# Values of sixteen meta tokens: both parts of the activations side by side as one stationary operand

## The chip, the cores and the metric

The kernel runs on one core of a Trainium2 chip. The metric is the device time in microseconds, taken as the median of several runs. TensorE multiplies matrices into PSUM, VectorE (DVE) and ScalarE (ACT) read PSUM and SBUF, GpSimd (POOL) reads SBUF alone, and DMA queues bring the weights from HBM.

## What is computed

A trunk of two layers over 16 learned meta tokens and 512 frames, each a vector of 1024. Each layer is a half-step feed-forward block, a mixer of three groups of heads (pooling, convolution, retention) and a second feed-forward block, each with a residual and a layer norm. The change is in the mixer, where the retention heads get their values `v` from the combined input projection:

```python
def token_mix(h, w_in, ..., w_out):
    z = h @ w_in
    xp, ca, cg, q, k, v, g = jnp.split(z, splits, axis=-1)
    y_pool = pool_mixer(xp, pool_w, pool_scale)
    y_conv = conv_module(ca, cg, conv_dw, conv_db, conv_ln_g, conv_ln_b, conv_pw)
    y_ret = retention(q, k, v, g, ret_gn_g)
    return jnp.concatenate([y_pool, y_conv, y_ret], axis=-1) @ w_out
```

In `retention` each of four heads of width 128 forms scores of `q` and `k` with decays, applies them to `v`, and normalizes the result over the head.

## The kernel before

All numbers are float32. For the matrix products each operand is split into a high part in fp32r and the remainder as a low part; a product is three matmuls: high by high, high by low and low by high (`mm3`, lines 130 to 135). `weights` (line 86) loads a block of weights, ScalarE casts the high part (line 91), VectorE subtracts it (line 94). Activations stand transposed: eight tiles `xs[k]` of 128 features, each in two halves of 264 columns (256 frames and 8 meta tokens), each half a pair of high and low part.

The mixer (`mixer`, from line 566) first projects the inputs of the convolution and of the pooling. Then it makes the values, the part that the change touches. `xm` gathers the meta tokens' 8 + 8 columns of both halves with small copies on GpSimd (line 670), four for each of eight feature tiles. Five passes over `tt` follow: four of 128 frames and, for `tt == 4`, one of the 16 meta tokens. A pass runs over eight feature tiles; the activations are the stationary operand, the weights' high and low parts the moving one of 512 columns, three matmuls for each tile (lines 680 to 682), 24 in a pass. Behind a pass VectorE sums the 512 columns of a row by heads (line 684) and scales by -1/128 (line 685), and ScalarE copies each head out of PSUM with that shift, four copies (line 690).

Then `work(hd, before)` makes, head by head, keys, gates and queries (`project`, `rotary`, lines 701 to 705). Each key half gives its 8 meta columns to the tile `km` by a copy on GpSimd (line 794). `attend` runs the score products (line 719; the first has `km` as its stationary operand), their decays (line 730), and the products with the values (line 738). Between these steps the 62 taps of the causal convolution are handed out on VectorE, one line 610 each, by the generator `conv_taps`, first asked for a tap within this loop.

The code's text isn't the order on the engines: a planner runs through the program with its own times for every instruction and puts on each engine, when that is free, the earliest instruction of the text whose inputs are there. That order is then fixed. Tiles of one tag share a number of buffers: `acc` has 4 PSUM banks (used by value passes, keys, queries and gates in turn), `wide` 16, the high and low parts of weights 5 each, `xm` 8.

Of the kernel before, what the change touches and what calls it, by code (L numbers as in the profile page):

```python
# [10 lines left out]
F32R = mybir.dt.float32r  # L11
I32 = mybir.dt.int32
AF = mybir.ActivationFunctionType
ALU = mybir.AluOpType
PSUM = bass.MemoryType.PSUM

P = 128
D = 1024
KT = D // P
SEQ = 512  # L20
NM = 16
# [24 lines left out]
HM = NM // 2  # L46
NT = 256 + HM
# [11 lines left out]
def trunk(ctx, tc, a):  # L59
    nc = tc.nc  # L60
# [3 lines left out]
    sq_pool = ctx.enter_context(tc.tile_pool(name="seqp", bufs=1))  # L64
    pp = ctx.enter_context(tc.tile_pool(name="pp", bufs=1, space=PSUM))

    def t(name, tag, dt=F32):
        return tp.tile([P, NT], dt, tag=tag, name=name, bufs=TILES[tag])

    def acc(name, tag="acc"):  # L70
        return pp.tile([P, 512], F32, tag=tag, name=name, bufs=BANKS[tag])
# [4 lines left out]
    def raw(r):  # L76
        return r.bitcast(F32)
# [42 lines left out]
    def wide(name, dt=F32):  # L120
        return sq_pool.tile([P, WIDE], dt, tag="wide", name=name, bufs=WIDES)
# [15 lines left out]
    def at(pair, sl):  # L137
        return pair[0][:, sl], pair[1][:, sl]
# [12 lines left out]
    xs = [[None, None] for _ in range(KT)]  # L151
# [214 lines left out]
    def project(ws, s, n, name):  # L366

        ps = [acc(f"{name}_{i}") for i in range(len(ws))]
        for k in range(KT):
            for w, p_ in zip(ws, ps):  # L370
                mm3(p_[:, :n], at(w, slice(k * P, (k + 1) * P)), at(xs[k][s], slice(0, n)), k == 0, k == KT - 1)
        return ps
# [193 lines left out]
    def mixer(l, name):  # L566
# [13 lines left out]
        for (kind, c), s in in_two([("u", 0), ("u", 1), ("xp", 0), ("xp", 1)], 3):  # L580
            n = ns[s]
            if s == 0:
                tiles = (c, 2 + c) if kind == "u" else (4 + c,)
                ws[kind, c] = [weights(w_in[i], 1024, f"{name}w{i}") for i in tiles]
                p_ = pad if kind == "u" else ppad
                seq[kind, c] = wide(f"{name}{kind}{c}")[:, : p_ + L]
                nc.gpsimd.memset(seq[kind, c][:, :p_], 0.0)  # L587
            ps = project(ws[kind, c], s, n, f"{name}p{kind}{c}{s}")
# [75 lines left out]

        xm = []
        for k in range(KT):
            pair = sq_pool.tile([P, 2, NM], F32R, tag="xm", name=f"{name}xm{k}", bufs=KT)
            for p_ in range(2):
                for s in range(2):
                    nc.gpsimd.tensor_copy(pair[:, p_, s * HM : (s + 1) * HM], raw(xs[k][s][p_][:, 256:NT]))  # L670
            xm.append((pair[:, 0, :], pair[:, 1, :]))
        vt = {}
        wv = [weights(a["w_v"][l, j], 1024, f"{name}wv{j}") for j in range(4)]
        for tt in range(5):
            n = NM if tt == 4 else P
            ps = acc(f"{name}v{tt}")
            for k in range(KT):
                xh, xl = xm[k] if tt == 4 else at(xs[k][tt // 2], slice(tt % 2 * P, (tt % 2 + 1) * P))
                wh, wl = at(wv[k // 2], slice((k % 2) * 512, (k % 2 + 1) * 512))
                nc.tensor.matmul(ps[:n], lhsT=xh, rhs=wh, start=k == 0, stop=False)  # L680
                nc.tensor.matmul(ps[:n], lhsT=xh, rhs=wl, start=False, stop=False)
                nc.tensor.matmul(ps[:n], lhsT=xl, rhs=wh, start=False, stop=k == KT - 1)
            mu = sq_pool.tile([P, HEADS], F32, tag="vmu", name=f"{name}vmu{tt}", bufs=2)
            nc.vector.tensor_reduce(out=mu[:n], in_=ps[:n].rearrange("p (h e) -> p h e", h=HEADS), axis=mybir.AxisListType.X, op=ALU.add)
            nc.vector.tensor_scalar(out=mu[:n], in0=mu[:n], scalar1=-1.0 / P, scalar2=None, op0=ALU.mult)
            for hd in range(HEADS):
                if hd % 2 == 0:
                    vc = t(f"{name}vc{tt}{hd}", "h")
                sl = slice((hd % 2) * P, (hd % 2 + 1) * P)
                nc.scalar.activation(vc[:n, sl], ps[:n, hd * P : (hd + 1) * P], AF.Identity, bias=mu[:n, hd : hd + 1])  # L690
                vt[tt, hd] = vc[:n, sl]
# [280 lines left out]
    for l in range(DEPTH):  # L972
        ffn(0, l, (NT, NT), f"f{l}a", V_LN + 3 * l * 16, {(1, 0): lambda: (load_tokens((2, 3, 5)), enter(1)), (0, 1): lambda: turn(1)} if l == 0 else {})
        if l == 0:
            with tc.issue_after(entered["ffn"]):
                load_mixer_constants()
        mixer(l, f"m{l}")
        if l < DEPTH - 1:
            ffn(1, l, (NT, NT), f"f{l}b", V_LN + (3 * l + 2) * 16)
        else:  # L980
            last_ffn(l, f"f{l}b")
# [92 lines left out]
```

## Time and profile before

| | us |
|---|---|
| median of 3 runs | 1978.54 |
| lowest and highest | 1976.29 and 1979.73 |
| profiled execution, its own time | 1979.3 |
| its span, first to last instruction | 1977.5 |
| TensorE busy | 1912.4 (97%) |
| VectorE busy | 1548.9 (78%) |
| ScalarE busy | 920.1 (47%) |
| GpSimd busy | 215.0 (11%) |

The prediction's rows come from the page of the profiled execution and from views of its trace: the waits (who waited for whom, and how long), the timeline (instructions of an engine in order of time, neighbours of one kind merged), and tables of busy time by stretches. Times count from the span's start. Layer 0's value passes lie at 427 to 455 us, layer 1's at 1405 to 1433. TensorE's weight loads (PEld) run beside its matmuls. A matmul's duration is longer than the distance to the next, since they are pipelined.

### The profile page before, as it was taken

How to read it: one execution, taken by the hardware profiler on the slowest of the kernel's cores; microseconds unless marked ns; L12 is line 12 of the kernel's file. 1: busy time of each engine (PE TensorE's matmuls, PEld its weight loads, DVE VectorE, ACT ScalarE, POOL GpSimd, SP SyncE). 2: the span in 40 equal slices, each digit the busy share in tenths (PEclk: the TensorE clock that was granted, in tenths of full speed). 3: DMA queues.
4: the chain of work that ended last, by engine and by line, in shares of the span. 5: the costliest groups of instructions: out<-in, count | busy, mean ns of one | idle time of the engine just before them, and what ended most of it. 6: DMA issues, size and time to landing. Idle time of an engine off the chain costs nothing.

```text
span 1977.5 us, 36739 instructions
## 1 busy us (share of the span) xinstructions
PE 1912.4 (97%) x14423; PEld 1826.3 (92%) x14423; DVE 1548.9 (78%) x3466; ACT 920.1 (47%) x1845; POOL 215.0 (11%) x283
## 2 busy tenths in 40 slices
PE   7999999999999999999999999999999999999996
PEld 6999999997899899999989999998889998999995
DVE  7788778689767977788697787787897697877787
ACT  5454446443333644454464554464343265544451
POOL 4000000442003000000120000005320130000001
PEclk9999999999999999999999999999999999999998
DMA  4422323322112233323213323332131213323321
GB/s 143 129 86 97 116 88 104 100 76 85 63 34 75 64 98 108 97 89 107 95 54 111 101 89 107 97 118 75 65 104 54 65 44 118 107 86 107 107 97 43
DMA packets 61069, 177.98 MB, mean 90 GB/s; under 512 B 6976, under 2 KB 10944, under 8 KB 60896
## 3 DMA queue, kind: packets, MB, share of 16 engines
q1 hardware_dynamic: 59744, 174.59, 27.8%
q8 instruction: 113, 1.85, 0.4%
q10 hardware_dynamic: 1152, 1.05, 0.2%
q14 instruction: 60, 0.49, 0.1%
HBM read 173.52 MB, written 2.10 MB: 89 GB/s over the span
## 4 chain that ended last, share of the span: by engine, by line
PE 79%; DVE 12%; POOL 3%; issue 3%; ACT 2%; DMA 0%; SPq 0%; DVEq 0%; POOLq 0%; ACTq 0%
PE f0a_y L134 2%; PE f0a_y L133 2%; PE f1bo L890 2%; PE f1bo L888 2%; PE f0a_y L135 2%; PE f1bo L889 2%; PE f0b_y L134 2%; PE f1a_y L134 2%; PE f0b_y L133 2%; PE f0b_y L135 2%; PE f1a_y L135 2%; PE f1a_y L133 2%; DVE m0y L610 1%; DVE m1y L610 1%; PE m0sc L719 1%
## 5 line engine op out<-in xcount | busy, mean ns | idle before, releaser
L610 DVE SCALAR_TENSOR_TENSOR m1y<-m1u,vec,m1y 128x528 f32<-128x528 f32 x60 | 46.1, 801 | 0.0
L91 ACT CAST f0a_o_h<-f0a_o_r 128x512 fp32r<-128x512 f32 (+1 forms) x37 | 23.5, 635 | 48.4 <-PE f0a_y L134 29.5
L610 DVE SCALAR_TENSOR_TENSOR m0y<-m0u,vec,m0y 128x528 f32<-128x528 f32 x60 | 45.9, 801 | 0.0
L91 ACT CAST f1a_o_h<-f1a_o_r 128x512 fp32r<-128x512 f32 (+1 forms) x37 | 23.6, 637 | 48.0 <-PE f1a_y L134 29.0
L91 ACT CAST f0b_o_h<-f0b_o_r 128x512 fp32r<-128x512 f32 (+1 forms) x37 | 23.5, 636 | 47.6 <-PE f0b_y L134 29.3
L335 DVE TENSOR_TENSOR x<-x,f0a_y 128x264 f32<-128x264 f32 x64 | 27.1, 425 | 23.3 <-PE f0a_y L135 23.1
L335 DVE TENSOR_TENSOR h<-h,f0b_y 128x264 f32<-128x264 f32 x64 | 27.1, 425 | 23.2 <-PE f0b_y L135 23.1
L335 DVE TENSOR_TENSOR h<-h,f1a_y 128x264 f32<-128x264 f32 x64 | 27.1, 424 | 23.1 <-PE f1a_y L135 23.0
L94 DVE TENSOR_TENSOR f1bw_l<-f1bw_r,f1bw_h 128x512 fp32r<-128x512 f32 x42 | 27.7, 688 | 17.6 <-ACT f1bw_h L91 17.0
L949 POOL TENSOR_TENSOR yt<-yt,g_last 128x256 f32<-128x256 f32 x4 | 3.0, 740 | 337.2 <-ACT yt L948 337.2
L94 DVE TENSOR_TENSOR f0a_o_l<-f0a_o_r,f0a_o_h 128x512 fp32r<-128x512 f32 (+1 forms) x42 | 26.6, 642 | 13.4 <-ACT f0a_o_h L91 11.3
L94 DVE TENSOR_TENSOR f1a_o_l<-f1a_o_r,f1a_o_h 128x512 fp32r<-128x512 f32 (+1 forms) x42 | 26.7, 642 | 13.4 <-ACT f1a_o_h L91 11.4
L94 DVE TENSOR_TENSOR f0b_o_l<-f0b_o_r,f0b_o_h 128x512 fp32r<-128x512 f32 (+1 forms) x42 | 26.7, 642 | 12.6 <-ACT f0b_o_h L91 10.4
L278 POOL TENSOR_TENSOR f0b_ln_s<-h,h 128x264 f32<-128x264 f32 x2 | 1.6, 820 | 313.8 <-DVE h L335 313.8
L587 POOL MEMSET m1u<- 128x30 f32 x2 | 0.2, 123 | 307.6 <-PE f1a_20Q L135 307.6
L587 POOL MEMSET m0u<- 128x30 f32 x2 | 0.2, 123 | 306.1 <-PE f0a_20Q L135 306.1
L91 ACT CAST f1bw_h<-f1bw_r 128x1024 fp32r<-128x1024 f32 (+1 forms) x22 | 22.2, 1011 | 21.0 <-PE f1bo L890 4.2
L894 DVE TENSOR_TENSOR yt<-yt,f1bo 128x256 f32<-128x256 f32 x80 | 27.8, 414 | 5.4 <-PE f1bo L890 5.3
L291 ACT ACTIVATE m_ln_q<-h 128x264 f32<-128x264 f32 (+1 forms) x32 | 11.9, 414 | 39.7 <-DVE h L289 36.1
L257 PE MATMUL tr<-ident,xtok 128*128 128x128 f32 (+1 forms) x48 | 10.9, 328 | 12.1 <-DVE xtok L242 11.4
L281 POOL TENSOR_TENSOR m_ln_s<-m_ln_s,h 128x264 f32<-128x264 f32 (+1 forms) x20 | 18.2, 912 | 32.0 <-DVE h L329 26.1
L257 PEld LDWEIGHTS tr<-ident,xtok 128*128 128x128 f32 (+1 forms) x48 | 6.8, 167 | 16.1 <-issue 14.8
(10805 smaller groups left out, 9335.0 us busy)
## 6 DMA issues: line engine op xcount, KB each, us to landing
f1bw_r<-in_w2last SPq DMA_DIRECT2D x20, 512.0 KB, 3.8
f0a_o_r<-in_w SPq DMA_DIRECT2D x32, 256.0 KB, 2.7
f0b_o_r<-in_w SPq DMA_DIRECT2D x32, 256.0 KB, 2.8
f1a_o_r<-in_w SPq DMA_DIRECT2D x32, 256.0 KB, 2.9
m0wo_r<-in_w_out SPq DMA_DIRECT2D x8, 512.0 KB, 3.5
m1wo_r<-in_w_out SPq DMA_DIRECT2D x8, 512.0 KB, 3.5
m0w_r<-in_w_in SPq DMA_DIRECT2D x6, 512.0 KB, 4.4
m1w_r<-in_w_in SPq DMA_DIRECT2D x6, 512.0 KB, 4.3
```

The costliest lines, as they stand in the source:

```text
L91: nc.scalar.copy(out=hi[:, :n], in_=w[:, :n])
L94: e.tensor_tensor(out=lo[:, sl], in0=w[:, sl], in1=raw(hi[:, sl]), op=ALU.subtract)
L133: nc.tensor.matmul(out, lhsT=wh, rhs=xh, start=start, stop=False, skip_group_check=onto)
L134: nc.tensor.matmul(out, lhsT=wh, rhs=xl, start=False, stop=False, skip_group_check=onto)
L135: nc.tensor.matmul(out, lhsT=wl, rhs=xh, start=False, stop=stop, skip_group_check=onto)
L335: nc.vector.tensor_tensor(out=y, in0=y, in1=ps, op=ALU.add)
L610: nc.vector.scalar_tensor_tensor(out=ys[c], in0=src, scalar=wk, in1=ys[c], op0=ALU.mult, op1=ALU.add)
L719: nc.tensor.matmul(sc[:kn, :cw], lhsT=kk[ks][:, kc : kc + kn], rhs=qq[s][:, c0 : c0 + cw], start=True, stop=True)
L888: nc.tensor.matmul(o, lhsT=hh, rhs=wh, start=part > 0 and i == 0, stop=False)
L889: nc.tensor.matmul(o, lhsT=hh, rhs=wl, start=False, stop=False)
L890: nc.tensor.matmul(o, lhsT=hl, rhs=wh, start=False, stop=i == nk - 1)
L894: nc.vector.tensor_tensor(out=y[:, :256], in0=y[:, :256], in1=o, op=ALU.add)
```

## The change

The tile of the meta tokens becomes one of 48 columns for each feature tile: 16 columns of the high part, 16 zeros (a memset on GpSimd), 16 columns of the low part. The pass for `tt == 4` then has two matmuls for each feature tile, one over the weights' high part and one over the low part, both with the 48 columns as stationary operand. Rows 0 to 15 of the result hold the high part's products, rows 32 to 47 the low part's. ScalarE copies the latter to a buffer `vm` of the tag `wide`, VectorE adds the former, and the sums and shifted copies read `vm` instead of PSUM. The product of both low parts is now in the sum as well. The other four passes are as they were.

```diff
         for k in range(KT):
-            pair = sq_pool.tile([P, 2, NM], F32R, tag="xm", name=f"{name}xm{k}", bufs=KT)
+            pair = sq_pool.tile([P, 48], F32R, tag="xm", name=f"{name}xm{k}", bufs=KT)
+            nc.gpsimd.memset(raw(pair[:, NM:32]), 0.0)
             for p_ in range(2):
                 for s in range(2):
-                    nc.gpsimd.tensor_copy(pair[:, p_, s * HM : (s + 1) * HM], raw(xs[k][s][p_][:, 256:NT]))
-            xm.append((pair[:, 0, :], pair[:, 1, :]))
+                    nc.gpsimd.tensor_copy(pair[:, 32 * p_ + s * HM : 32 * p_ + (s + 1) * HM], raw(xs[k][s][p_][:, 256:NT]))
+            xm.append(pair)
...
             for k in range(KT):
-                xh, xl = xm[k] if tt == 4 else at(xs[k][tt // 2], slice(tt % 2 * P, (tt % 2 + 1) * P))
                 wh, wl = at(wv[k // 2], slice((k % 2) * 512, (k % 2 + 1) * 512))
+                if tt == 4:
+
+                    nc.tensor.matmul(ps[:48], lhsT=xm[k], rhs=wh, start=k == 0, stop=False)
+                    nc.tensor.matmul(ps[:48], lhsT=xm[k], rhs=wl, start=False, stop=k == KT - 1)
+                    continue
+                xh, xl = at(xs[k][tt // 2], slice(tt % 2 * P, (tt % 2 + 1) * P))
...
+            if tt == 4:
+                vm = wide(f"{name}vm")
+                nc.scalar.copy(out=vm[:n, :512], in_=ps[32 : 32 + n])
+                nc.vector.tensor_tensor(out=vm[:n, :512], in0=ps[:n], in1=vm[:n, :512], op=ALU.add)
+                ps = vm[:, :512]
```

## Rows read from the trace of the kernel before

**Rows 1.** Waits of TensorE: engine, line, waited for: us in total, times, longest.

```profile
PE m1sc L719 <- POOL m1km L794: 3.5, 1, 3.5
```

**Rows 2.** Timeline of TensorE, layer 0: start, duration, line, operation, out<-in, shapes.

```profile
449.67 0.40 PE L680 MATMUL m0v<-m0wv_h,m0xm 128*16 128x512 f32 x1
...
454.97 0.40 PE L682 MATMUL m0v<-m0wv_h,m0xm 128*16 128x512 f32 x1
455.21 0.28 PE L133 MATMUL m0kp<-f0a_ln_x0h,m0wk_h 128*128 128x264 f32 x1
...
472.56 0.28 PE L135 MATMUL m0kp<-f0a_ln_x7h,m0wk_l 128*128 128x264 f32 x1
476.23 1.06 PE L719 MATMUL m0sc<-m0q00r,m0km 128*16 128x264 f32 x2 [3.38 <-POOL m0km L794]
```

**Rows 3.** Stretches: length, busy PE, PEld, DVE, ACT, POOL, clock, DMA, GB/s.

```profile
427.00:472.80 45.80, 45.80 (x269) 38.07 (x267) 45.80 (x77) 17.36 (x41) 14.53 (x9) 1.00 0.26 84
472.80:476.20 3.40, 0.05 (x1) 0.00 (x0) 3.40 (x9) 1.80 (x4) 3.38 (x1) 0.86 0.01 4
476.20:482.20 6.00, 5.97 (x23) 4.93 (x24) 6.00 (x15) 1.23 (x1) 1.94 (x2) 0.51 0.29 90
482.20:540.00 57.80, 57.79 (x409) 51.85 (x408) 45.74 (x132) 18.54 (x38) 2.91 (x6) 1.00 0.18 55
...
1450.80:1454.30 3.50, 0.00 (x0) 0.00 (x0) 3.50 (x9) 1.83 (x4) 3.45 (x1) 1.00 0.21 26
1454.30:1458.40 4.10, 4.09 (x16) 3.32 (x17) 4.10 (x11) 1.15 (x1) 1.60 (x1) 0.58 0.31 110
```

**Rows 4.** Timeline of GpSimd, the copies into km, layers 0 and 1.

```profile
466.44 3.76 POOL L794 COPY m0km<-m0k00r 128x8 f32<-128x8 f32 x1 [29.06 <-DVE m0k00r L705]
470.14 6.03 POOL L794 COPY m0km<-m0k01r 128x8 f32<-128x8 f32 x1
...
1448.26 5.99 POOL L794 COPY m1km<-m1k01r 128x8 f32<-128x8 f32 x1
```

**Rows 5.** Timeline of VectorE, layer 0 and one row of layer 1.

```profile
450.23 0.68 DVE L684 TENSOR_REDUCE m0vmu<-m0v 128x4 f32<-128x512 f32 x1
450.83 0.75 DVE L610 SCALAR_TENSOR_TENSOR m0y<-m0u,vec,m0y 128x528 f32<-128x528 f32 x1
...
451.57 4.16 DVE L610 SCALAR_TENSOR_TENSOR m0y<-m0u,vec,m0y 128x528 f32<-128x528 f32 x6
455.65 0.68 DVE L684 TENSOR_REDUCE m0vmu<-m0v 128x4 f32<-128x512 f32 x1
...
457.68 1.28 DVE L94 TENSOR_TENSOR m0wq_l<-m0wq_r,m0wq_h 128x512 fp32r<-128x512 f32 x2
...
459.56 1.28 DVE L94 TENSOR_TENSOR m0wk_l<-m0wk_r,m0wk_h 128x512 fp32r<-128x512 f32 x2
460.77 0.67 DVE L684 TENSOR_REDUCE m0vmu<-m0v 16x4 f32<-16x512 f32 x1
...
473.57 0.41 DVE L703 TENSOR_TENSOR m0q01r<-m0qp,cosb 128x264 f32<-128x264 f32 x1
...
475.80 0.41 DVE L703 TENSOR_TENSOR m0k10r<-m0kp,cosb 128x264 f32<-128x264 f32 x1
...
479.53 0.41 DVE L703 TENSOR_TENSOR m0k11r<-m0kp,cosb 128x264 f32<-128x264 f32 x1
...
1453.89 0.41 DVE L703 TENSOR_TENSOR m1k10r<-m1kp,cosb 128x264 f32<-128x264 f32 x1
```

**Rows 6.** Instructions on the tile m0v: count, shortest, median, longest ns, first and last start.

```profile
L680 PEld LDWEIGHTS m0v<-m0wv_h,m0xm x8: 94/95/95, 449.4 to 454.3; 128*16 128x16 f32 x8
...
L680 PEld LDWEIGHTS m0v<-m0wv_h,f0a_ln_x0h x4: 188/188/188, 427.2 to 443.9; 128*128 128x128 f32 x4
```

**Rows 7.** Timeline of ScalarE, a copy of 64x535 in layer 0.

```profile
434.98 0.64 ACT L641 COPY m0sm<-m0sm 64x535 f32<-64x535 f32 x1 [6.12 <-POOL m0sm L642]
```

**Rows 8.** Instructions of line 587: a memset of the mixer, columns as in rows 6.

```profile
L587 POOL MEMSET m1u<- x2: 123/123/123, 1329.5 to 1329.8; 128x30 f32 x2
```

## What it does to the time

> **What bounds the kernel now.** The table of busy time by engine comes first: TensorE works through nearly all of the span, so work taken from it can count, but only where it does not have to wait right afterwards. The table of waits answers that: among TensorE's longest is one of 3.5 us in layer 1's mixer, where the first score product (line 719) waits for GpSimd's copy into km (line 794) [rows 1], and its like in layer 0 took 3.38 us [rows 2]. Both come after the value passes that the change touches. The timeline of TensorE puts layer 0 in order: the pass for the meta tokens begins at 449.67 and its last matmul at 454.97; the key and query products then run back to back until the one that begins at 472.56; then TensorE stands until 476.23 [rows 2]. The table by stretches shows who is behind: from 427 to 482.2 VectorE is busy in every microsecond, also in the 3.40 us in which TensorE does nothing, and the same stands in layer 1 [rows 3]. Last, GpSimd's timeline: two copies of 128x8 took 3.76 and 6.03 us, and the second ended at 470.14 + 6.03 = 476.17 [rows 4], when VectorE was ending line 703 for k10 (475.80 + 0.41 = 476.21), an operation that reads PSUM [rows 5]. So the restart of TensorE hangs on the place of that line 703 in VectorE's queue, and VectorE has no gap ahead of it. In this stretch VectorE sets the time, not TensorE.
>
> **TensorE's part.** The pass goes from 24 matmuls to 16. 24 matmuls start within (454.97 - 449.67) / 23 = 0.230 us of each other [rows 2]; eight fewer are 1.84 us a layer, 3.69 us for two. The wider stationary operand costs nothing that I can see: a load of 16 columns took 94 ns and one of 128 took 188 ns [rows 6], so 48 columns lie between, and both are below the 230 ns of the matmul that covers them. Without that cover 16 loads would cost at most 16 x 0.1 us more.
>
> The step back from 16 to 128 columns took 455.21 - 454.97 = 0.24 us, as long as any step within the pass [rows 2]. The Trainium skill (TensorEngine Tiling, Key Properties) says that a change of tiling mode drains TensorE. Here no drain shows at 16 columns, and no run shows 48; if one came, a matmul would end (0.40 us) before the next begins instead of 0.23 us, 0.17 us for each of two changes, and the pass would give 1.50 us a layer instead of 1.84.
>
> **What it adds.** On ScalarE a copy of 16x512 out of PSUM: the nearest row, 64x535, took 0.64 us [rows 7]. On VectorE one addition of 16x512: the reduction of the same shape took 0.67, and two line 94 of 128x512 took 1.28, so about 0.64, between 0.60 and 0.68 [rows 5]. The reduction and the four shifted copies read SBUF instead of PSUM; no row shows these shapes from there, and I take them as unchanged, give or take 0.1 us. On GpSimd eight memsets a layer of 128x16; one of 128x30 took 123 ns, and those of layer 1 ran from 1329.5, some 120 us ahead of that layer's score product at 1454.3 [rows 3, 8]. The new ones have no input either, so I expect them in gaps of GpSimd, for nothing. If they stood just ahead of the 32 small copies instead, they would cost GpSimd 8 x 0.12 = 1 us at a time when TensorE is busy with projections. The two new steps hold things up in their queues: the copy holds up, on ScalarE, the casts of wk, wg and wq behind it, for which VectorE's line 94 waits (for wk at 459.56 [rows 5]): 0 to 0.64 us. The addition holds up all of VectorE's later rotary work: 0.64 us. The wide buffer that the copy takes is one of 16; I expect no wait for it. The bank of the pass comes free right after the addition, earlier than after four shifted copies, which can only help.
>
> **Where the 1.84 us go.** TensorE reaches the score product 1.84 us earlier, and only waits longer, unless VectorE's line 703 for k10 comes earlier too. Its place in the queue was not written by hand. The code asks for the first convolution tap only after all value passes, yet taps stand between the reductions: from 450.23 to 455.65 one reduction, then seven taps (one and six) and a tiny scaling [rows 5]. That is 5.4 us of VectorE for one pass of 24 x 0.230 = 5.5 us of TensorE. So the planner that orders the queue expects the pass to last that long and fills the time with taps; it should see the shorter pass too and put fewer taps ahead of the rotary work. Between the reductions at 455.65 and 460.77 there are three taps and four line 94 [rows 5], and more taps up to 475.80, so there are enough to leave out. A tap adds 0.68 us (six in 4.16 us, which includes an end of 0.07). Filled time shrinks by 1.84 while 0.64 is new in it, so 3 or 4 taps step out: 3 x 0.68 - 0.64 = 1.40 us, or 4 x 0.68 - 0.64 = 2.08 us earlier. The taps that leave go behind: from 482.2 to 540 VectorE is busy 45.7 of 57.8 us [rows 3], which hides 2 to 3 us more. The middle is 1.74; with a part of ScalarE's push I take 1.6 us a layer. TensorE's wait then stays at about 3.4 to 3.7 us, and everything from the score product on is 1.6 us earlier.
>
> The sum against the profiled execution: 1979.3 (span 1977.5, and 1.8 around it) - 2 x 1.6 = 1976.1. That execution lay 0.76 us above the median of the runs, so the forecast is 1978.54 - 3.2 = 1975.3. What a measurement of this kernel can tell from no change is about 0.2%, that is 4 us: 1974.6 to 1982.5. The whole of what is removed, 3.7 us, lies inside it.
>
> **The rivals.**
> *The order of VectorE stays.* Then VectorE gets 0.64 us a layer more ahead of line 703 for k10, TensorE's wait grows from 3.4 to 5.9 us, and the gain is gone: + 1.3 us, 1979.8, with up to 1 us a layer more if the copy's push on the casts comes on top (1982). For it: VectorE is saturated. Against it: the count of taps, above.
>
> *GpSimd's copy misses its place* (the slower side). The long copy ended with a VectorE operation that reads PSUM in both layers: in layer 1 at 1448.26 + 5.99 = 1454.25, and line 703 for k10 at 1453.89 + 0.41 = 1454.30 [rows 4, 5]. The taps and splits ahead of it read two SBUF operands. If the new order lets the second copy miss line 703 for k10, the next of its kind is that for k11, 479.53 + 0.41 = 479.94, which is 3.73 us later [rows 5]. A layer would then be 3.73 - 1.6 = 2.1 us slower, both 4.3: 1982.8. It decides when the second copy starts after line 703 for q01 has begun. One layer alone gives 1979.1. The Trainium skill (SBUF — State Buffer, Who interferes with whom) says the same: a VectorE instruction with two SBUF inputs blocks a GpSimd instruction that reads SBUF. The trace agrees for these copies: 6.03 us for 128x8 [rows 4].
>
> *The clock does not fall.* After the wait the granted clock was 0.51 for 6.0 us in layer 0 and 0.58 for 4.1 us in layer 1 [rows 3], the lower level of 1.2 GHz for most of it. That costs 6.0 x 0.49 = 2.9 us and 4.1 x 0.42 = 1.7 us. If the new order ends the copy one place earlier, at line 703 for q01 (473.57 instead of 475.80 [rows 5]), the wait is cut by 2.23 us and the clock may stay: 2.23 and 2.9 or 1.7, so 4 to 5 us in a layer beside the 1.6. Both layers would be near 1966, one near 1971. Speaking for it: the copies' luck with places goes both ways; against it: TensorE arrives 1.84 us earlier, which lengthens the wait.
>
> **How the numbers follow.** Re-planned order, 1.4 to 2.1 us a layer (1974.3 to 1975.7, to 1977 with the whole push on top): 0.55, of which 0.08 is past 0.2%. Order stays: 0.17 (1978.5 to 1982). Copy misses its place: 0.13, of which 0.11 past 0.2% slower. Clock or place gained: 0.15, all faster. So faster 0.23, slower 0.13 (0.02 from the order that stays), the same 0.64. The range takes in all but the two-layer ends of the last rivals: 1971.0 to 1982.0.
>
> **What would show it.** In the new profile: 16 matmuls in the pass, next product at about 453.4 in layer 0; three or four taps fewer between the reduction of v3 and line 703 for k10, which starts near 474.2; TensorE's wait for km still 3 to 4 us in each layer; taps ending later. Wrong would be: the same count of taps ahead of line 703 (the order stays), a copy into km that ends at another place, a stretch of low clock that is gone or twice as long, or memsets in a row ahead of the copies. The prediction fails as a whole if the re-planning also moves work in the feed-forward stages, whose orders I take as unchanged.

## The result, and the profile after

The changed kernel takes 1999.49 us (median, 1994.54 to 2006.88) where the kernel before, run on the same chip, takes 1978.93 (1976.29 to 1979.73). The ratio is 1.0107, 95% interval 1.0085 to 1.0128: 20 us slower, where 3 us faster was forecast. The profiled execution of the changed kernel is the longest of its runs (2006.88 us, span 2005.1), so its stages show some 7 us more than the median. Line numbers behind the change have moved: the reduction is now L695, the addition of the two parts L692, the rotary work L714 to L716, the copies into km L805, the score products L730, their decays L741.

The waits of TensorE (engine, line, waited for: us in total, times, longest) show where the time went. The waits for km of [rows 1] and [rows 2] are gone, and these stand in their place:

```profile
PE m0sc L730 <- DVE m0sm L741: 12.6, 3, 10.0
PE m1sc L730 <- DVE m1sm L741: 12.3, 3, 8.4
```

TensorE's timeline in layer 0 (start, duration, line, operation, the last brackets: idle before and what ended it) puts the longest of them in its place. The first two score products run as soon as TensorE reaches them; the third needs the PSUM bank that the first holds (their tag `att` has two) until VectorE has applied its decay (line 741):

```profile
472.06 0.60 PE L730 MATMUL m0sc<-m0q00r,m0km 128*16 128x264 f32 x2 [0.28 <-DVE m0q00r L716]
472.60 0.70 PE L730 MATMUL m0sc<-m0q00r,m0k00r 128*128 128x256 f32 x2
...
485.05 0.80 PE L730 MATMUL m0sc<-m0q00r,m0k00r 128*128 128x128 f32 x2 [10.04 <-DVE m0sm L741]
```

That decay on VectorE:

```profile
484.58 0.41 DVE L741 TENSOR_TENSOR m0sm<-m0sc,decm 16x264 f32<-16x264 f32 x1
```

Why VectorE is so late is seen 30 us earlier. Its timeline through the value passes, layer 0 and two rows of layer 1:

```profile
445.08 0.69 DVE L695 TENSOR_REDUCE m0vmu<-m0v 128x4 f32<-128x512 f32 x1 [4.75 <-PE m0v L688]
...
450.66 0.69 DVE L695 TENSOR_REDUCE m0vmu<-m0v 128x4 f32<-128x512 f32 x1 [4.68 <-PE m0v L688]
...
457.10 0.67 DVE L692 TENSOR_TENSOR m0vm<-m0v,m0vm 16x512 f32<-16x512 f32 x1
457.70 0.53 DVE L608 TENSOR_SCALAR m0y<-m0u,vec 128x528 f32<-128x528 f32 x1
...
1447.65 0.67 DVE L692 TENSOR_TENSOR m1vm<-m1v,m1vm 16x512 f32<-16x512 f32 x1
1448.25 0.53 DVE L608 TENSOR_SCALAR m1y<-m1u,vec 128x528 f32<-128x528 f32 x1
```

Between the reductions, where seven taps stood in [rows 5], VectorE now idles 4.7 us. The first tap of a layer (L608) comes directly behind the addition into `vm`, in both layers. In the kernel before it ran ahead of the value passes:

```profile
424.76 0.55 DVE L608 TENSOR_SCALAR m0y<-m0u,vec 128x528 f32<-128x528 f32 x1
```

So some 33 us in which taps could run are lost, and the taps crowd into the stretch in which the rotary work and the decays are due: from 457 us to the first decay there are 22 of them, in the kernel before 13. The table of stretches shows both halves (length, busy PE, PEld, DVE, ACT, POOL, clock, DMA, GB/s), first one row of the kernel before:

```profile
400.00:450.00 50.00, 49.97 (x319) 45.06 (x318) 40.99 (x79) 17.91 (x41) 18.02 (x34) 1.00 0.22 75
```

then those of the changed one:

```profile
400.00:450.00 50.00, 49.95 (x322) 45.37 (x322) 20.12 (x51) 18.59 (x44) 7.23 (x24) 1.00 0.24 75
...
478.00:484.00 6.00, 0.00 (x0) 0.00 (x0) 6.00 (x14) 0.00 (x0) 1.30 (x2) 0.57 0.00 0
484.00:490.00 6.00, 4.96 (x16) 3.97 (x17) 6.00 (x11) 0.39 (x1) 0.03 (x1) 0.50 0.26 90
490.00:500.00 10.00, 10.00 (x59) 8.09 (x59) 6.97 (x18) 2.18 (x5) 0.00 (x0) 0.88 0.18 52
490.00:547.00 57.00, 55.23 (x364) 49.36 (x364) 48.01 (x135) 17.25 (x35) 1.11 (x2) 0.92 0.15 47
```

From 400 to 450 VectorE is busy 20 us instead of 41; from 478 to 490 it has no gap. The clock falls to the lower level (0.57 and 0.50 of full speed, 1.2 GHz for most of it) while TensorE stands still, and is back at the upper one only at 492.5 us, 7.4 us after the restart (hence the 0.88 from 490 to 500, a part of the last row). A second stretch at the lower level lies between 516 and 524 us. In layer 0 the stretch from the first value matmul to the first matmul of the output projection grows from 141.5 to 153.4 us, by 11.9. Three terms account for that: TensorE stands idle for 12.9 instead of 3.4 us (+ 9.5); the low clock, counted in steps of half a microsecond and only where TensorE is busy, costs 7.1 instead of 2.9 us (+ 4.2); eight matmuls are gone (- 1.8): + 11.9. Layer 1 grows by 13.1 (+ 9.2, + 5.7, - 1.8). The rest of the span grows by some 2.6 us.

### The profile page after: what moved, and what is told of

Same layout as the page of the kernel before. It is cut to its first block, busy times and chain, and to the rows that moved or that the text cites. A ratio compares the mean times of both kernels' runs of the same rounds, so it can differ in the third digit from the quotient of the medians.

```text
span 2005.1 us, 36704 instructions
## 1 busy us (share of the span) xinstructions
PE 1920.3 (96%) x14407; PEld 1833.0 (91%) x14407; DVE 1547.0 (77%) x3468; ACT 921.2 (46%) x1847; POOL 193.8 (10%) x299
## 5 line engine op out<-in xcount | busy, mean ns | idle before, releaser
L291 ACT ACTIVATE m_ln_q<-h 128x264 f32<-128x264 f32 (+1 forms) x32 | 11.9, 414 | 40.4 <-DVE h L289 36.9
L257 PE MATMUL tr<-ident,xtok 128*128 128x128 f32 (+1 forms) x48 | 10.9, 328 | 12.2 <-DVE xtok L242 11.7
```

What stands on the lines that cost most here:

```text
L257: nc.tensor.transpose(out=ps[:, c0 : c0 + p], in_=y[m // 4][:, m % 4 * P : (m % 4 + 1) * P], identity=ident[:p, :p])
L291: nc.scalar.activation(q[i][:, :n], y[:, :n], AF.Square)
```

## The experiments

Three theories were on the table. **A**: the buffer. `vm` asks for one of the 16 `wide` buffers; the two tiles `y` of the taps and the pooling windows' tiles ask for theirs further down in the text. (To ask means here the first instruction that writes the tile: `y` is named at line 600, above `vm`, but first written by the first taps, below it.) If buffers of a tag are granted in the order of the text, `y` gets none before `vm` has, and `vm` is first written when the last value pass is done. **B**: the memsets. They can be seen on GpSimd ahead of the pooling windows, in the changed kernel at 451 us, waiting for the value pass of layer 0 because they clear the tiles for layer 1:

```profile
451.08 0.11 POOL L668 MEMSET m1xm<- 128x16 f32 x1 [39.30 <-PE m0v L683]
...
454.41 0.11 POOL L668 MEMSET m1xm<- 128x16 f32 x1 [0.42 <-PE m0v L683]
454.46 0.66 POOL L639 COPY m0sm<-m0xp 128x1 f32<-128x1 f32 x1
455.08 1.55 POOL L642 TENSOR_TENSOR m0sm<-m0xp 128x542 f32<-128x542 f32 x1
```

The windows (L642) had run at 423 to 437 us in the kernel before. Against B from the start: layer 1 has no such memsets and its taps are as late. **C**: the added steps cost by their own length, some 0.6 us each.

**The wide buffer alone**, put into the kernel before; the meta tokens' pass keeps its 24 matmuls:

```diff
+            if tt == 4:
+                vm = wide(f"{name}vm")
+                nc.scalar.copy(out=vm[:n, :512], in_=ps[:n])
+                ps = vm[:, :512]
             mu = sq_pool.tile([P, HEADS], F32, tag="vmu", name=f"{name}vmu{tt}", bufs=2)
```

> The kernel before, with its 24 matmuls, three for each feature tile, and without memsets; the one thing added is that the meta tokens' values go through a buffer of the tag wide (a ScalarE copy of 16x512 out of PSUM, then the sums and shifted copies read it). Theory A (the planner grants buffers of one tag in the order of the text, so a wide buffer that is first written only after the meta pass holds back the taps' and the pooling windows' wide buffers, which stand later in the text): the first tap (line 608) starts only after the meta pass in both layers, TensorE waits some 8 to 12 us at the score products in each layer, and the time is 15 to 25 us above before, 1994 to 2004. Theory B (the memsets for the next layer's meta tile block GpSimd's queue): no memsets here, so 1978 to 1981. Theory C (the added steps cost by their own length): at most 0.6 us a layer on ScalarE, 1978 to 1981.

Measured: 1999.22 us (1996.21 to 1999.96), ratio 1.0092 (1.0076 to 1.0108). Its VectorE begins with the taps behind the reduction of `vm`, and its TensorE waits at the score products:

```profile
455.97 0.67 DVE L688 TENSOR_REDUCE m0vmu<-m0vm 16x4 f32<-16x512 f32 x1
456.57 0.53 DVE L608 TENSOR_SCALAR m0y<-m0u,vec 128x528 f32<-128x528 f32 x1
```

```profile
PE m1sc L723 <- DVE m1sm L734: 9.2, 3, 3.6
PE m0sc L723 <- DVE m0sm L734: 7.3, 3, 3.4
```

This buffer alone makes a loss of 19 us, with neither memsets nor the two-matmul pass in the kernel, so A stands and C, which gave 1978 to 1981 here, falls. The wait in layer 0, 7.3 us, is a little under the 8 to 12 expected. The pooling windows (L642) ran at 422 to 434 us, as early as before: it is the late taps that cost.

**The zeros once**: the changed kernel, its `xm` tiles made and cleared at the start of the program.

```diff
+    xm_all = []
+    for k in range(KT):
+        xm_all.append(sq_pool.tile([P, 48], F32R, tag="xm", name=f"xm{k}", bufs=KT))
+        nc.gpsimd.memset(raw(xm_all[k][:, NM:32]), 0.0)
...
-            pair = sq_pool.tile([P, 48], F32R, tag="xm", name=f"{name}xm{k}", bufs=KT)
-            nc.gpsimd.memset(raw(pair[:, NM:32]), 0.0)
+            pair = xm_all[k]
```

> The changed kernel, with the eight meta tiles made once at the start of the program and zeroed there, so that no memset stands in GpSimd's queue between the layers' work. Theory A: taps still late in both layers, 1988 to 2000, at most some us better than the changed kernel. Theory B: layer 0 gets back what it lost, about half of the 20 us: 1985 to 1990. Theory C: no difference to the changed kernel, 1997 to 2002.

Measured: 1998.52 us (1997.50 to 2002.87), ratio 1.009 (1.0071 to 1.0108). The loss stays; B falls as its cause. What the memsets had held up is seen too: the first pooling window starts at 423.4 us again, the first tap at 456.5.

**Another tag**: the changed kernel with `vm` in two buffers of the tag `sm` of 256 columns each, so with two copies, two additions and two reductions of 16x256.

```diff
-                vm = wide(f"{name}vm")
-                nc.scalar.copy(out=vm[:n, :512], in_=ps[32 : 32 + n])
-                nc.vector.tensor_tensor(out=vm[:n, :512], in0=ps[:n], in1=vm[:n, :512], op=ALU.add)
-                ps = vm[:, :512]
+                for j in range(2):
+                    vm = t(f"{name}vm{j}", "sm")[:, :256]
+                    c = slice(j * 256, (j + 1) * 256)
+                    nc.scalar.copy(out=vm[:n], in_=ps[32 : 32 + n, c])
+                    nc.vector.tensor_tensor(out=vm[:n], in0=ps[:n, c], in1=vm[:n], op=ALU.add)
+                    halves.append((vm, 2 * j, 2))
```

> The changed kernel, with its 16 matmuls and its memsets; the low part's copy goes to two buffers of 256 columns of the tag sm (first asked for later in the text by the score products) instead of one of the tag wide, so one copy, one addition and one reduction more, each on half the columns. Theory A: the taps stand between the value passes again, TensorE's wait at the score products is that of the kernel before (3 to 4 us a layer), and the time is 1974 to 1979. Theory B: the memsets are still there, and layer 0 stays slow: 1985 to 1990. Theory C: about 2000, as the changed kernel.

and the same with the zeros once:

> Both edits together: two buffers of the tag sm, and the meta tiles zeroed once at the start of the program. Theory A: the same as with the other tag alone, within 3 us, 1974 to 1979. Theory B: all of the loss gone, and 8 to 12 us below the kernel with the other tag alone. Theory C: about 2000. If the re-planning of my prediction holds once the taps are in place, line 703 for k10 starts 1.4 to 2.1 us earlier than before after the value passes, and the time is 2 to 4 us below before.

Measured: 1978.72 us (1975.75 to 1982.66), ratio 0.9993 (0.9982 to 1.0003), and with the zeros once 1978.91 (1975.08 to 1985.96), ratio 0.9995 (0.9984 to 1.0007), both beside 1979.98 for the kernel before. The loss is gone, and the memsets cost nothing that these runs can tell. But 3.7 us of matmuls are gone as well, and of the 2 to 4 us that the last expectation had from them about 1 has come, which is not clear of no change at all. VectorE's and TensorE's timelines of the first of the two show why:

```profile
454.27 0.67 DVE L700 TENSOR_REDUCE m0vmu<-m0v 128x4 f32<-128x512 f32 x1
...
472.52 0.43 DVE L720 TENSOR_TENSOR m0k10r<-m0kp,cosb 128x264 f32<-128x264 f32 x1
...
475.50 0.41 DVE L747 TENSOR_TENSOR m0sm<-m0sc,decm 16x264 f32<-16x264 f32 x1
```

```profile
469.60 0.62 PE L736 MATMUL m0sc<-m0q00r,m0km 128*16 128x264 f32 x2
...
475.97 0.80 PE L736 MATMUL m0sc<-m0q00r,m0k00r 128*128 128x128 f32 x2 [4.39 <-DVE m0sm L747]
```

From the reduction of v3 to the rotary work of k10 VectorE needs 472.52 - 454.27 = 18.25 us; before it was 475.80 - 455.65 = 20.15 [rows 5]. That is 1.9 us, inside the 1.4 to 2.1 of the prediction, and in the program's order on VectorE 42 taps instead of 46 stand ahead of the first decay. The first score product no longer waits at all. The third does, for the decay, 4.4 us instead of 3.4.

**Two taps first**: is it the place in the text or is a buffer short? The changed kernel, whole, its `wide` buffer and memsets included; two of 62 taps are asked for ahead of the value passes.

```diff
+        taps = conv_taps()
+        for _ in range(2):
+            next(taps)
+
         xm = []
...
-        taps = conv_taps()
         pool_y = {}
```

> The changed kernel as it is, its wide buffer and its memsets included; only the first two taps (one for each of the two tiles y) are asked for in the text ahead of the value passes instead of behind them. The tiles y then ask for their wide buffers before vm does. The planned order has 44 taps ahead of the first decay in layer 0 and 43 in layer 1, where the kernel before has 46 and the changed one 22. Theory A (buffers of a tag are granted in the order of the text, so vm, asked for early and written late, holds back whoever asks later): the loss goes, 1976 to 1981. Rival (one wide buffer too few: vm occupies one that others need, wherever it stands in the text): 1995 to 2000, as the changed kernel. The pooling windows still ask for theirs behind vm; if that alone is enough for half of the loss: about 1990.

Measured: 1979.75 us (1976.40 to 1986.75) beside 1979.35 for the kernel before, ratio 1.000 (0.999 to 1.001). With the same 16 buffers the loss of 20 us is gone. Its first tap starts at 414.17 us; the next ones are early too:

```profile
419.93 0.55 DVE L608 TENSOR_SCALAR m0y<-m0u,vec 128x528 f32<-128x528 f32 x1
...
423.40 4.84 DVE L610 SCALAR_TENSOR_TENSOR m0y<-m0u,vec,m0y 128x528 f32<-128x528 f32 x7
```

No buffer was short: it was who asked first. The line that names `y` was not moved, only its first writes. The pooling windows still stand behind the memsets in layer 0 (the first L642 at 454.17 us); no cost of it shows in the median, though in the profiled execution TensorE's wait for a decay is 5.2 us there and 3.5 in layer 1.

**The copies into km on ScalarE**, in the kernel before: does GpSimd hold TensorE up there, or VectorE's backlog?

```diff
-                    nc.gpsimd.tensor_copy(km[:, s * HM : (s + 1) * HM], kq[0][s][:, 256:NT])
+                    nc.scalar.copy(out=km[:, s * HM : (s + 1) * HM], in_=kq[0][s][:, 256:NT])
```

> The kernel before, with the two copies into km on ScalarE instead of GpSimd; nothing of the change is in it. The planned order keeps 46 taps ahead of VectorE's first decay, as before. Theory 1 (VectorE's backlog sets TensorE's restart, and the long copy on GpSimd is only the wait that ends last): the first score product starts some 3 us earlier, but the third has to wait for a bank of the tag att, which VectorE's decay of the first score frees at about 477 us in layer 0, so a wait of 4 to 5 us stands there instead of the one of 3.4 us, with the low clock behind it: 1978 to 1982. Rival (GpSimd's copy alone holds TensorE up): both waits of 3.4 us go, and the stretches of 6.0 and 4.1 us at half the clock with them, 2.9 and 1.7 us: 1980 - 6.8 - 4.6 = 1968.6, between 1967 and 1972.

Measured: 1983.39 us (1978.95 to 1987.89), ratio 1.0018 (1.0008 to 1.0028), a little above what theory 1 allowed and far from the rival. The wait moved:

```profile
472.83 0.62 PE L719 MATMUL m0sc<-m0q00r,m0km 128*16 128x264 f32 x2
473.38 0.70 PE L719 MATMUL m0sc<-m0q00r,m0k00r 128*128 128x256 f32 x2
...
479.38 0.80 PE L719 MATMUL m0sc<-m0q00r,m0k00r 128*128 128x128 f32 x2 [4.57 <-DVE m0sm L730]
```

GpSimd's copy of 6.03 us was the last link of the chain, not its length. Without it the next link, the decay, is as late. TensorE's idle time of 4.6 instead of 3.4 and 3.5 us accounts for 2.3 of the 4 us that this run is slower; where the rest comes from is not shown.

**Taps held back**: from the 29th on they may not be issued before VectorE's first decay of the layer. First in the kernel before:

```diff
+                    if 2 * k + c == 28:
+                        held.append(decayed[0])
...
-                        nc.vector.scalar_tensor_tensor(out=ys[c], in0=src, scalar=wk, in1=ys[c], op0=ALU.mult, op1=ALU.add)
+                        with tc.issue_after(held[0]) if held else nullcontext():
+                            nc.vector.scalar_tensor_tensor(out=ys[c], in0=src, scalar=wk, in1=ys[c], op0=ALU.mult, op1=ALU.add)
```

> The kernel before, with the taps from the 29th on held back on VectorE until the first decay has been issued; nothing of the change is in it. The planned order has 28 taps ahead of the first decay instead of 46: 18 x 0.68 = 12 us of VectorE's work leave the stretch in which TensorE ends up waiting. Theory 1 (VectorE's backlog sets TensorE's restart): the waits of 3.4 us at the score products go, and the stretches of low clock behind them, worth 2.9 and 1.7 us: 6.8 + 4.6 = 11.4 us at most, 1969; where the held taps come back as new waits further on (VectorE was busy 45.7 of 57.8 us between 482 and 540, so about 12 us of idle time stand against 12 us of taps), half of it: 1974. Rival (the wait is GpSimd's own, or TensorE's other waits grow by as much): 1978 to 1984.

and then with the change in it (two buffers of the tag `sm`, the zeros once):

> The change with its intermediate sum in two smaller buffers of another tag and with the zeros written once, as in e4_other_tag_zero_once, and with the taps from the 29th on held back as in e8_before_hold. VectorE's planned order is that of e8_before_hold but for the sum of the two parts. If VectorE no longer sets TensorE's restart, the eight matmuls that each layer saves show in full against e8_before_hold: 2 x 1.84 = 3.7 us less, so 1965 to 1970 if that run gives 1969 to 1974. Rival (the saving only lengthens a wait, as in e4_other_tag_zero_once, which gained 1 us): the same time as e8_before_hold within 1.5 us.

Measured: the kernel before with held taps 1967.53 us (1965.45 to 1971.99), ratio 0.9940 (0.9926 to 0.9953); with the change as well 1963.92 (1963.88 to 1964.32), ratio 0.9918 (0.9905 to 0.9932), the fastest of all. The held taps alone gave 11.8 us, where 11.4 was expected at the most; with the change it is 3.6 us more, expected 3.7. Neither has a wait of TensorE at a score product. The timeline of TensorE, first the kernel before with held taps, then the one with the change:

```profile
473.19 0.62 PE L724 MATMUL m0sc<-m0q00r,m0km 128*16 128x264 f32 x2
473.74 0.70 PE L724 MATMUL m0sc<-m0q00r,m0k00r 128*128 128x256 f32 x2
474.52 0.38 PE L724 MATMUL m0sc<-m0q00r,m0k00r 128*128 128x128 f32 x2
```

```profile
470.13 0.62 PE L745 MATMUL m0sc<-m0q00r,m0km 128*16 128x264 f32 x2
470.68 0.70 PE L745 MATMUL m0sc<-m0q00r,m0k00r 128*128 128x256 f32 x2
471.46 0.38 PE L745 MATMUL m0sc<-m0q00r,m0k00r 128*128 128x128 f32 x2
```

And the stretches of the one with the change:

```profile
470.10:476.00 5.90, 5.90 (x38) 4.71 (x38) 5.12 (x11) 3.47 (x5) 0.19 (x1) 1.00 0.08 33
476.00:482.00 6.00, 6.00 (x43) 5.20 (x42) 4.85 (x12) 1.28 (x2) 0.00 (x0) 1.00 0.00 0
482.00:540.00 58.00, 57.92 (x407) 52.15 (x406) 53.73 (x149) 19.04 (x40) 4.28 (x6) 1.00 0.18 57
```

TensorE has no gap, the clock stays at 1.00, and the held taps fill VectorE from 482 to 540 (53.7 of 58 us, before 45.7 of 57.8 [rows 3]) without a new wait.

From the first value matmul to the first of the output projection, in the profiled executions, in us:

| kernel | layer 0 | layer 1 |
|---|---|---|
| before | 141.5 | 138.0 |
| changed | 153.4 | 151.1 |
| before with the wide buffer alone | 148.2 | 148.7 |
| changed, zeros once | 147.6 | 147.6 |
| changed, another tag | 139.5 | 137.5 |
| changed, another tag, zeros once | 139.7 | 140.3 |
| changed, two taps first | 143.2 | 138.1 |
| before, km copies on ScalarE | 141.6 | 139.4 |
| before, taps held | 135.3 | 132.4 |
| changed, another tag, zeros once, taps held | 133.5 | 130.6 |

Each line is one execution, and the low clock alone moves these lengths: in layer 1 of the two kernels with another tag TensorE stands idle for 4.8 us in both, but the low clock costs 1.6 us in one and 4.8 in the other. The last two lines have neither idle time (under 0.1 us) nor low clock, so they can be compared. They differ by 1.8 us in each layer: the price that the prediction had put on eight matmuls (1.84), paid in full once VectorE does not set TensorE's restart. The medians differ by 3.6 us.

## Why the prediction was wrong

**The step that failed** is the sentence "The wide buffer that the copy takes is one of 16; I expect no wait for it." It counted buffers, and asked whether the copy would wait for one. The question was who would then wait behind the copy. The prediction itself noted that the taps run ahead of their place in the text, and that from 450.23 on they fill VectorE between the reductions. They can do that only if their two tiles `y` already have a buffer. A request for the same tag, earlier in the text and filled only after the last value pass, took that away: the wide buffer alone in the kernel before cost 19 us, and two taps moved ahead of it in the text gave all of the changed kernel's loss back. That the planner grants buffers in the order of first writes is inferred from these runs. None of the rivals had this. The rival on the slower side (a copy into km that misses its place) was another mechanism, and did not occur: those copies became shorter (0.66 and 0.60 us in layer 0 of the changed kernel).

**Right, with sizes.** The pass of 16 matmuls: 1.8 us less in each layer, forecast 1.84. ScalarE's copy 0.58 us, forecast 0.64; the addition 0.67, forecast 0.64; the load of the stationary operand 122 ns, between the 94 and 188 of [rows 6]. Of the instructions on the tile `m0v` (count, shortest, median, longest ns, first and last start):

```profile
L682 PEld LDWEIGHTS m0v<-m0wv_h,m0xm x8: 121/122/122, 450.2 to 453.4; 128*48 128x48 f32 x8
```

and of the instructions on the tile `m0vm`:

```profile
L691 ACT COPY m0vm<-m0v x1: 577/577/577, 455.3 to 455.3; 16x512 f32<-16x512 f32 x1
L692 DVE TENSOR_TENSOR m0vm<-m0v,m0vm x1: 671/671/671, 457.1 to 457.1; 16x512 f32<-16x512 f32 x1
```

The step from the 48-column pass to the next product takes as long as a step within the pass:

```profile
452.31 0.40 PE L692 MATMUL m0v<-m0wv_l,xm 128*48 128x512 f32 x1
452.55 0.28 PE L133 MATMUL m0kp<-f0a_ln_x0h,m0wk_h 128*128 128x264 f32 x1
```

So 48 columns show no more of a drain than 16 did. The Trainium skill (TensorEngine Tiling (Array Packing), Key Properties) says that a change of tiling mode drains TensorE; the step of 0.24 us does not show one here.

The memsets: for nothing in time, as forecast, but not "in gaps". The prediction took them to wait for nothing; but they clear buffers that the value pass of layer 0 still reads. In the changed kernel those of layer 1 stand for 39 us in GpSimd's queue with the pooling windows of layer 0 behind them. With the taps in place this shows in no median: 1979.75 us with two taps first, beside 1979.35 before. With another tag the memsets come behind the windows and cost nothing measurable either (1978.72 us, 1978.91 without them).

**The re-planning** was right where the buffer did not hinder it (another tag): three taps stepped out between the reduction of v3 and the rotary work of k10 in layer 0 (8 instead of 11), four ahead of the first decay, and that rotary work came 1.9 us earlier, forecast 3 or 4 taps and 1.4 to 2.1 us.

**A second step would have failed too.** "TensorE's wait then stays at about 3.4 to 3.7 us": with the buffer under another tag it is 4.4 to 4.5 us, at the third score product instead of the first. The reading of the profile had the right engine (VectorE is full) but took the last link, line 703 and GpSimd's copy, as the one place to watch. Behind it stood the decays, just as late in the same queue. So even without the buffer the forecast of 3.2 us would have come out at about 1.

**The price of the backlog** was in the rows. The two waits (3.4 and 3.5 us) and the low clock behind them (2.9 and 1.7) add to 11.5 us, and holding the taps back gave 11.8. The prediction worked these numbers out only as a rival of a lucky place.

What stays open: the changed kernel's layer 0 is 5.8 us longer in its profiled execution than with the zeros once, while the runs of these two kernels (medians 1999.49 and 1998.52) overlap. Some 4 us of it are low clock (7.1 instead of 3.1), which differs as much in layer 1, where no memsets stand and the idle times agree (12.8 and 12.9). The other 2 us are idle time (12.9 instead of 10.9); whether the memsets cause these was not settled.

## What to carry to other kernels

Before a change takes a buffer from a shared tag, ask when that buffer is first written and who further down in the text asks for the same tag: a tile that asks early and is filled late holds back everything that was meant to run ahead. When a wait ends with a full engine, look at what comes next in that engine's queue before counting on the wait: moving the last link (the copies into km) only showed the next one. Work that fills gaps is better held back by hand until the urgent work has been issued; only then did eight saved matmuls show as 1.8 us in both layers.

## What was not expected of the hardware

GpSimd's copy of 128x8 took 3.76 and 6.03 us in the kernel before [rows 4]. With the taps held back, so that none stood beside it, the same copy took 0.53 and 0.19 us (with another tag and taps beside it 1.27 and 0.59); GpSimd's timeline with the change and held taps, layer 0:

```profile
460.78 0.53 POOL L821 COPY m0km<-m0k00r 128x8 f32<-128x8 f32 x1 [24.22 <-DVE m0k00r L731]
464.22 0.19 POOL L821 COPY m0km<-m0k01r 128x8 f32<-128x8 f32 x1 [2.92 <-DVE m0k01r L731]
```

It goes the other way too. In the changed kernel, where the pooling windows ran late, a VectorE subtraction of 128x512 that takes 0.64 us in [rows 5] took 1.58 beside GpSimd's L642 (455.08 to 456.63, above):

```profile
455.60 1.58 DVE L94 TENSOR_TENSOR m0wg_l<-m0wg_r,m0wg_h 128x512 fp32r<-128x512 f32 x1
```

The Trainium skill (SBUF — State Buffer, Who interferes with whom) says that a VectorE instruction with two SBUF inputs contends with a GpSimd one that reads SBUF, and that the order of issue decides who blocks. These rows agree with contention in both directions; no run here separates the port from another cause. Nor do they show why a copy should wait through a dozen VectorE instructions: line 703 for q01, at 473.57 in [rows 5], reads PSUM as well and lies inside the copy of 6.03 us, which the prediction's account of these copies leaves open.
